# A retention layer and its MLP: every fourth weight block's low parts are made by an accumulating transfer

## The chip, the cores and the metric

The kernel runs on one core of a Trainium2 chip. The metric is device time in microseconds (us) of one launch. The core has five engines that run side by side and wait for one another by semaphores: TensorE (PE in the profile, PEld for its weight loads), VectorE (DVE), ScalarE (ACT), GpSimd (POOL) and SyncE (SP). Sixteen DMA engines move data; a transfer is started by an instruction in the queue of SP, ACT or POOL.

## The reference

With `DEPTH = 1` the program is one retention layer and one squared-ReLU MLP, on 256 tokens of width 2048 in float32:

```python
hn = rmsnorm(x, norm1)
q, k, v, g = split(hn @ w_in)            # 8 heads, 256 wide (q, k), 512 wide (v, g)
q, k = rotary(q), rotary(k) * DK ** -0.5
o = decayed causal attention of q, k, v in chunks of 64 positions
o = head_norm(o, gn_gain, center=True) * silu(g)
x = x + o @ w_out
x = x + square(relu(rmsnorm(x, norm2) @ w_up)) @ w_down    # 8192 wide
out = rmsnorm(x, final_norm)
```

All weights together are 256 blocks of 1 MiB, and each is read once.

## The kernel before, in words

The result has float32 accuracy although TensorE is fed numbers of type float32r. So each weight block is split in a rounded part and a residue: `wh` is the block rounded to float32r by ScalarE (line 59), `wl` is the raw block minus `wh`, by VectorE (line 60). The activations are split likewise, and each product is three matmul passes: `wh` with the activations' high part, `wl` with their high part, `wh` with their low part.

`load_block` does this for one block. SP starts one transfer of 1 MiB into `raw` (128 partitions x 2048 numbers, three buffers in rotation). The block is split in two halves of 128 x 1024; each half has its own `wh` and `wl`, of which there are four buffers each. So the split of half h can begin when TensorE has finished with half h - 4, that is when it starts on half h - 3. Only the first four blocks (head 0's gates) are loaded and split in pieces, with `lead`.

Two loops use the blocks. `proj_cols` (queries and keys, `w_up`) holds the weights stationary: a half is 2 row tiles x 4 column groups, with one matmul of 512 columns on `wh` (line 82) and one of 256 on `wl` (line 83) in each. `proj_rows` (gates, values, `w_o`, `w_down`) holds the activations stationary: a half is 12 matmuls of 512 columns, on `wh` (line 97), on `wl` (line 98), and again on `wh` (line 101). With `late=4`, in the very last projection, the last four row tiles (two blocks, four halves) are kept back and used accumulator by accumulator, so that all four halves are needed within the first twelve matmuls.

The order is: for each of 8 heads four blocks of gates, four of queries and keys, four of values; then two times 16 blocks of `w_o`; then two times 32 blocks of `w_up` and 32 of `w_down`. Between the blocks stand the rest of the layer: `mix` (scores times values), `turn` (transposes, split into `ys` by line 147), the norms. GpSimd does little: the first sums of squares, the reciprocal roots (line 143), and it starts two transfers, the residual `x` (2 MiB, line 325) and `fnorm` (1 MiB, line 392). `x` can start only when the buffers that it takes over are free, at the last head's `turn` after block 4 of `w_o`.

The instructions of each engine run in the order in which the scheduler of the framework has put them, which need not be the order of the code.

Of the kernel before, what the change touches and what calls it, by code (L numbers as in the profile page):

```python
# [9 lines left out]
F32 = mybir.dt.float32  # L10
F32R = mybir.dt.float32r
AF = mybir.ActivationFunctionType
ALU = mybir.AluOpType
PSUM = bass.MemoryType.PSUM

P = 128
T = 256
D = 2048
# [7 lines left out]
EPS = 1e-6  # L26
# [3 lines left out]

@with_exitstack
def trunk_kernel(ctx: ExitStack, tc: tile.TileContext, io, out):
    """One retention layer and its squared-ReLU MLP.

    Every weight product is three float32r passes over exact 12-bit parts (w = wh + wl,
    x = xh + xl): wh*xh + wh*xl + wl*xh, accumulated in float32.
    """
    nc = tc.nc

    cp = ctx.enter_context(tc.tile_pool(name="cp", bufs=1))  # L40
# [3 lines left out]
    def bank(name):  # L44
        return ps.tile([P, 512], F32, tag="bank", name=name)

    # ---- weights: a block of 1 MiB, loaded whole and split in two halves; or, row tile by
    # row tile, with lead(row tile) before each ----
    def load_block(src, rows, cols, lead=None):
        raw = wp.tile([P, 2048], F32, tag="raw", name="raw", bufs=3)  # L50
        if lead is None:
            nc.sync.dma_start(raw, src)
        parts = []
        for s in range(2):
            wh = wp.tile([P, 1024], F32R, tag="wh", name="wh", bufs=4)
            wl = wp.tile([P, 1024], F32R, tag="wl", name="wl", bufs=4)
            r = raw[:, s * 1024 : (s + 1) * 1024]
            if lead is None:
                nc.scalar.copy(wh, r)  # L59
                nc.vector.tensor_sub(wl, r, wh.bitcast(F32))  # L60
            for k in range(rows // 2):
                sl = slice(k * cols, (k + 1) * cols)
                if lead is not None:
                    row = s * rows // 2 + k
                    lead(row)
                    nc.sync.dma_start(r[:, sl], src[:, row * cols : (row + 1) * cols])
                    nc.scalar.copy(wh[:, sl], r[:, sl])  # L67
                    nc.vector.tensor_sub(wl[:, sl], r[:, sl], wh[:, sl].bitcast(F32))  # L68
                parts.append((wh[:, sl], wl[:, sl]))
        return parts  # L70

    # weights stationary: acc[o][n, t] (xh) and acc[o][n, T + t] (xl) over the rows of w,
    # o = 0..3 blocks of 128 columns
    def proj_cols(src, xs, accs, fillers=()):
        for g in range(KT // 4):
            parts = load_block(src[g], 4, 512)
            for j, (wh, wl) in enumerate(parts):
                kt = 4 * g + j
                for o, acc in enumerate(accs):
                    c = slice(o * P, (o + 1) * P)  # L80
                    both = xs[:, kt].rearrange("p a t -> p (a t)")
                    nc.tensor.matmul(acc, wh[:, c], both, start=(kt == 0), stop=False)  # L82
                    nc.tensor.matmul(acc[:, :T], wl[:, c], xs[:, kt, 0, :], start=False, stop=(kt == KT - 1))  # L83
            for f in [f for at, f in fillers if at == g]:
                f()

    # activations stationary: accs[b][c][t, n] over nk row tiles, two token blocks; the last
    # `late` row tiles go to one accumulator after another, with done(b, c) behind each
    def proj_rows(blocks, per, xs, accs, nk, after=(), late=0, done=None, lead=None):
        nch = len(accs[0])  # L90
        kept = []
# [26 lines left out]
                if done:  # L118
                    done(b, c)

# [1 line left out]
    xs = cp.tile([P, KT, 2, T], F32R, tag="xs", name="xs")  # L122
    xr = cp.tile([P, KT, T], F32, tag="ys", name="xr", padded_shape=[P, VT * 2, T])
    norm1 = cp.tile([P, KT], F32, name="norm1")
# [6 lines left out]
    nc.vector.memset(ones, 1.0)  # L131
    nc.vector.memset(mhalf, -0.5)

    # while the first loads are under way: the activation table, and the tensor engine's clock
    warm = cp.tile([P, 1], F32, name="warm")
    nc.scalar.activation(warm, ones[:, 0:1], AF.Silu)
    pw = bank("pw")
# [1 line left out]
        nc.tensor.matmul(pw[:, :P], ones, ones, start=True, stop=True)  # L139

    def rsqrt(r, v):
        """r = v ** -0.5 for [P, 1] tiles."""
        nc.gpsimd.tensor_tensor(r, v, mhalf, op=ALU.pow)

    def split_scaled(dst, src, scale):
        """dst[:, 0] + dst[:, 1] = src * scale, scale [P, 1]."""
        nc.scalar.activation(dst[:, 0, :], src, AF.Copy, scale=scale)
        nc.vector.scalar_tensor_tensor(
            dst[:, 1, :], src, scale, dst[:, 0, :].bitcast(F32), op0=ALU.mult, op1=ALU.subtract
        )  # L150

    with tc.tile_pool(name="ap", bufs=1) as ap:
        # x transposed, times norm1, in two parts; sums of squares by token
        sq = ap.tile([P, 4, T], F32, name="sq")
        sqs = ap.tile([P, T], F32, name="sqs")
        cosr = ap.tile([P, T], F32, name="cosr")
# [3 lines left out]
        def load_x(k0, n):  # L160
            ks = slice(k0, k0 + n)
            nc.sync.dma_start(xr[:, ks], io["xT"][:, ks])
            for k in range(k0, k0 + n):
                split_scaled(xs[:, k], xr[:, k], norm1[:, k : k + 1])

        def lead_x(k):
            """x ahead of the first weights: row tile by row tile, then four at once."""
            if k < 4 or k % 4 == 0:
                load_x(k, 1 if k < 4 else 4)

# [30 lines left out]
            nc.vector.tensor_mul(cosr, cosr, rsrow)  # L201
            nc.vector.tensor_mul(sinr, sinr, rsrow)

# [1 line left out]
        st = {}  # L205

        def gates(h, after, lead=None):
# [38 lines left out]
            st["v"] = v  # L246

        def scores(h):
            """Decayed scores, keys on partitions: columns 0..255 keys 0..127, 256..383 keys 128..255."""
            qk = st["qk"]  # L250
            pst = bank("pst")
            for b in range(NB):
                q = slice(b * P, T)
                to = slice(0, T) if b == 0 else slice(T, T + P)
                for i in range(2):
                    nc.tensor.matmul(
                        pst[:, to], qk[:, 1, i, b * P : (b + 1) * P], qk[:, 0, i, q], start=(i == 0), stop=(i == 1)
                    )
            sd = ap.tile([P, 384], F32, tag="sd", name="sd")
            sh = ap.tile([P, 384], F32R, tag="sh", name="sh")  # L260
            sl = ap.tile([P, 384], F32R, tag="sl", name="sl")
            nc.vector.tensor_mul(sd[:, :T], pst[:, :T], dec[:, h])
            nc.vector.tensor_mul(sd[:, T:384], pst[:, T:384], dec[:, h, :P])
            nc.scalar.copy(sh, sd)
            nc.vector.tensor_sub(sl, sd, sh.bitcast(F32))
            st["s"] = sh, sl
# [49 lines left out]
                nc.sync.dma_start(dec, io["dec"])  # L316
            values(h, [(1, lambda h=h: scores(h))])

# [1 line left out]
        acc0 = [[bank("acc_o") for _ in range(2)] for _ in range(NB)]  # L320
        proj_rows(io["w_o"][0], 2, ys, acc0, VT, [(1, lambda: mix(H - 1)), (4, lambda: turn(H - 1))])

# [1 line left out]
    x = mp.tile([P, NB, D], F32, name="x")  # L324
# [4 lines left out]
    ms2 = mp.tile([P, NB], F32, name="ms2")  # L329
# [10 lines left out]
        )  # L340

    def partial_sum(b):
        """ms2 = the first three sums + D * EPS"""
        m = ms2[:, b : b + 1]
        nc.vector.tensor_scalar(m, ss[:, b, 0:1], ss[:, b, 1:2], D * EPS, op0=ALU.add, op1=ALU.add)
        nc.vector.tensor_add(m, m, ss[:, b, 2:3])
# [40 lines left out]
            nc.tensor.matmul(psr[:, b * P : (b + 1) * P], ones, dg2[:, b], start=True, stop=True)  # L387
        nc.vector.tensor_copy(rsrow2, psr[:, :T])

# [1 line left out]
    fnorm = mp.tile([P, D], F32, name="fnorm")  # L391
    nc.gpsimd.dma_start(fnorm, io["final_norm"])
    rs3 = mp.tile([P, NB], F32, name="rs3")
# [21 lines left out]
    for fh in range(2):  # L415
        hs = cp.tile([P, VT, 2, T], F32R, tag="ys", name="hs")
        for c in range(8):
            acc = [bank("acc_u") for _ in range(4)]
            proj_cols(io["w_up"][8 * fh + c], x1s, acc, [(1, second_norm)] if fh == 0 and c == 0 else ())
            for o in range(4):  # L420
                t = mp.tile([P, T], F32, tag="t", name="t", bufs=3)
                s = mp.tile([P, T], F32, tag="s", name="s", bufs=3)
# [7 lines left out]
        for half in range(2):  # L430
            acc = [[bank("acc_d") for _ in range(2)] for _ in range(NB)]
            last = fh == 1
            proj_rows(
                io["w_down"][fh][half], 2, hs, acc, VT,
                late=4 if last and half == 1 else 0,
                done=(lambda b, c: finish(b, half, c)) if last else (lambda b, c: add_residual(acc, half, b, c)),
# [1 line left out]


def _tables():  # L440
    """Rotary and decay tables: functions of the shapes alone."""
    f = np.float32
    inv = f(10000.0) ** (-np.arange(0, DK, 2, dtype=f) / f(DK))
    ang = np.arange(T, dtype=f)[None, :] * inv.astype(f)[:, None]
    cos, sin = np.cos(ang).astype(f), np.sin(ang).astype(f)
    lg = np.log1p(-np.exp2(-5.0 - np.arange(H, dtype=np.float64)))
    j, i = np.arange(P)[:, None], np.arange(T)[None, :]
    seen = (j // CHUNK) <= (i // CHUNK)
    dist = np.abs(i - j)
    dec = np.exp(lg[None, :, None] * dist[:, None, :]) * seen[:, None, :] * DK**-0.5  # L450
    return cos, sin, np.ascontiguousarray(dec.astype(f))


def _blocks(w, rows, cols):
    """[K, N] -> [N / cols, K / (128 rows), 128, rows, cols], each block contiguous."""
    k, n = w.shape
    w = w.reshape(k // (P * rows), rows, P, n // cols, cols).transpose(3, 0, 2, 1, 4)
    return np.ascontiguousarray(w).reshape(n // cols, k // (P * rows), P, rows * cols)
# [44 lines left out]
```

## Time and profile before

| what | value |
|---|---|
| time, median of 2 runs | 1492.38 us (1492.07 to 1492.69) |
| span of the profiled execution, first to last instruction | 1491.0 us |
| median less span (what lies around the span) | 1.4 us |
| TensorE matmuls, busy | 1471.6 us (99%) |
| VectorE, busy | 852.9 us (57%) |
| ScalarE, busy | 675.8 us (45%) |
| GpSimd, busy | 40.3 us (3%) |
| SP's transfers | 274.05 MB, 52.2% of the 16 DMA engines' time |

No time of the profiled execution other than its span is recorded, so sums are made against the span and 1.4 us are added. "Busy" counts the time in which an instruction of that engine is running; a matmul's end is modelled, and matmuls overlap, so the distance from start to start tells the pace. "idle before <- releaser" names what an engine waited for.

### The profile page before, as it was taken

To read this page: it belongs to the slowest core of one execution; us is meant where nothing else is said; L and a number is where in the kernel's file an instruction comes from. 1 tells how busy PE (TensorE), PEld (TensorE's weight loads), DVE (VectorE), ACT (ScalarE), POOL (GpSimd) and SP (SyncE) were. 2 spreads that over 40 slices of the span, in tenths; PEclk is the share of its full clock that TensorE was granted. 3 is DMA by queue.
4 is the path that set the end of the run, shared out by engine and by line. 5 is a ranking of instruction groups with operands and counts; after the bars stand their busy time and mean duration, and the time that the engine had idled before them with its cause. 6 is when DMAs were issued, how large, how long until landed. Compare 5 with 4: busy or idle time off the path is not lost.

```text
span 1491.0 us, 17881 instructions
## 1 busy us (share of the span) xinstructions
PE 1471.6 (99%) x7172; PEld 1233.2 (83%) x7172; DVE 852.9 (57%) x1099; ACT 675.8 (45%) x870; POOL 40.3 (3%) x48
## 2 busy tenths in 40 slices
PE   7999999999999999999999999999999999999997
PEld 5888888888888888888888888888888888888885
DVE  8656565656565656546466566544446566554645
ACT  5444444444444444434345455533334555443332
POOL 6000000000000000000000000000000000000000
PEclk8999999999999999999999999999999999999999
DMA  6654454454445445655555555555555555555552
GB/s 235 225 187 182 170 198 170 170 188 179 173 174 191 172 174 191 254 198 175 192 175 192 178 189 190 181 194 196 192 185 189 194 176 195 180 189 195 198 185 98
DMA packets 42260, 278.35 MB, mean 187 GB/s; under 512 B 5056, under 2 KB 5952, under 8 KB 9408
## 3 DMA queue, kind: packets, MB, share of 16 engines
q1 hardware_dynamic: 41616, 274.05, 52.2%
q0 software_dynamic: 416, 3.15, 0.5%
q8 instruction: 56, 0.92, 0.2%
q14 instruction: 28, 0.23, 0.0%
q10 hardware_dynamic: 144, 0.01, 0.0%
HBM read 275.09 MB, written 2.10 MB: 186 GB/s over the span
## 4 chain that ended last, share of the span: by engine, by line
PE 96%; DVE 1%; DMA 1%; issue 1%; ACT 0%; POOL 0%; SPq 0%; POOLq 0%; ACTq 0%; DVEq 0%
PE acc_u L82 16%; PE acc_qk L82 8%; PE acc_u L83 8%; PE acc_d L101 8%; PE acc_d L97 8%; PE acc_d L98 8%; PE acc_qk L83 4%; PE acc_v L101 4%; PE acc_v L97 4%; PE acc_v L98 4%; PE acc_o L97 4%; PE acc_o L101 4%; PE acc_g L101 4%; PE acc_o L98 4%; PE acc_g L98 4%; PE acc_g L97 4%
## 5 line engine op out<-in xcount | busy, mean ns | idle before, releaser
L60 DVE TENSOR_TENSOR wl<-raw,wh 128x1024 fp32r<-128x1024 f32 x504 | 615.6, 1224 | 600.9 <-ACT wh L59 600.8
L59 ACT CAST wh<-raw 128x1024 fp32r<-128x1024 f32 x504 | 529.8, 1051 | 703.6 <-PE acc_d L101 204.4
L82 PE MATMUL acc_u<-x1s,wh 128*128 128x512 f32 x1024 | 362.1, 398 | 0.0
L83 PE MATMUL acc_u<-x1s,wl 128*128 128x256 f32 x1024 | 287.8, 281 | 0.0
L82 PEld LDWEIGHTS acc_u<-x1s,wh 128*128 128x128 f32 x1024 | 192.5, 188 | 47.4
L97 PE MATMUL acc_d<-wh,hs 128*128 128x512 f32 x512 | 200.0, 391 | 0.0
L98 PE MATMUL acc_d<-wl,hs 128*128 128x512 f32 x512 | 199.9, 390 | 0.0
L83 PEld LDWEIGHTS acc_u<-x1s,wl 128*128 128x128 f32 x1024 | 192.2, 188 | 0.0
L82 PE MATMUL acc_qk<-xs,wh 128*128 128x512 f32 x512 | 182.1, 398 | 0.0
L101 PE MATMUL acc_d<-wh,hs 128*128 128x512 f32 x512 | 160.8, 393 | 0.0
L83 PE MATMUL acc_qk<-xs,wl 128*128 128x256 f32 x512 | 143.9, 281 | 0.0
L82 PEld LDWEIGHTS acc_qk<-xs,wh 128*128 128x128 f32 x512 | 96.3, 188 | 23.1
L98 PEld LDWEIGHTS acc_d<-wl,hs 128*128 128x128 f32 x512 | 96.1, 188 | 22.2 <-DVE wl L60 0.3
L101 PEld LDWEIGHTS acc_d<-wh,hs 128*128 128x128 f32 x512 | 96.2, 188 | 20.8
L97 PEld LDWEIGHTS acc_d<-wh,hs 128*128 128x128 f32 x512 | 96.2, 188 | 20.4
L98 PE MATMUL acc_g<-wl,xs 128*128 128x512 f32 x256 | 101.9, 398 | 7.5 <-DVE wl L68 7.5
L97 PE MATMUL acc_g<-wh,xs 128*128 128x512 f32 x256 | 101.9, 401 | 0.5 <-ACT wh L67 0.5
L101 PE MATMUL acc_g<-wh,xs 128*128 128x512 f32 x256 | 102.1, 399 | 0.0
L97 PE MATMUL acc_v<-wh,xs 128*128 128x512 f32 x256 | 100.8, 394 | 0.0
L101 PE MATMUL acc_v<-wh,xs 128*128 128x512 f32 x256 | 100.6, 393 | 0.0
L97 PE MATMUL acc_o<-wh,ys 128*128 128x512 f32 x256 | 100.6, 393 | 0.0
L98 PE MATMUL acc_o<-wl,ys 128*128 128x512 f32 x256 | 100.0, 391 | 0.0
(96 smaller groups left out, 1279.5 us busy)
## 6 DMA issues: line engine op xcount, KB each, us to landing
raw<-in_w_up SPq DMA_DIRECT2D x64, 1024.0 KB, 4.9
raw<-in_w_down SPq DMA_DIRECT2D x64, 1024.0 KB, 4.9
raw<-in_w_qk SPq DMA_DIRECT2D x32, 1024.0 KB, 4.9
raw<-in_w_v SPq DMA_DIRECT2D x32, 1024.0 KB, 4.9
raw<-in_w_o SPq DMA_DIRECT2D x32, 1024.0 KB, 4.9
raw<-in_w_g SPq DMA_DIRECT2D x28, 1024.0 KB, 4.9
raw<-in_w_g SPq DMA_DIRECT2D x16, 256.0 KB, 6.3
x<-in_x POOLq DMA_DIRECT2D x1, 2048.0 KB, 10.4
```

Of the source, the lines that this page charges most:

```text
L59: nc.scalar.copy(wh, r)
L60: nc.vector.tensor_sub(wl, r, wh.bitcast(F32))
L82: nc.tensor.matmul(acc, wh[:, c], both, start=(kt == 0), stop=False)
L83: nc.tensor.matmul(acc[:, :T], wl[:, c], xs[:, kt, 0, :], start=False, stop=(kt == KT - 1))
L97: nc.tensor.matmul(accs[b][c], xs[:, kt, 0, t], wh[:, n], start=(kt == 0), stop=False)
L98: nc.tensor.matmul(accs[b][c], xs[:, kt, 0, t], wl[:, n], start=False, stop=False)
L101: nc.tensor.matmul(accs[b][c], xs[:, kt, 1, t], wh[:, n], start=False, stop=(kt == nk - 1))
```

## The change

The fourth, eighth, twelfth block and so on (blocks 8, 12, ..., 256 of the 256, since block 4 is loaded with `lead`) makes `wl` in another way: ScalarE writes the raw half times -1, rounded to float32r, into `wl`, and GpSimd starts a transfer that adds the raw half onto it, tile to tile within the core's own memory. These are 63 blocks, the last of each group of four: 126 halves. The negation reads `raw`, not `wh`. The other 378 halves are split as before. The diff, without the comments that it also drops:

```diff
+    count = [0]
+
     def load_block(src, rows, cols, lead=None):
+        count[0] += 1
+        by_dma = lead is None and count[0] % 4 == 0
         raw = wp.tile([P, 2048], F32, tag="raw", name="raw", bufs=3)
...
             if lead is None:
                 nc.scalar.copy(wh, r)
-                nc.vector.tensor_sub(wl, r, wh.bitcast(F32))
+                if by_dma:
+                    nc.scalar.activation(wl, r, AF.Copy, scale=-1.0)
+                    nc.gpsimd.dma_start(out=wl, in_=r, accum_op=ALU.add)
+                else:
+                    nc.vector.tensor_sub(wl, r, wh.bitcast(F32))
```

In the changed file the cast stands on line 63, the negation on line 65, the transfer on line 66; lines behind are moved by 8. On SP nothing is moved; on PE four rows in `w_down`'s last blocks are.

GpSimd's queue before, from the first norm (line 143, `rs`) over the eight heads (`rv`, two in each) to the end:

```order
L143 TENSOR_TENSOR rs<-ms,mhalf 128x1 x2
L143 TENSOR_TENSOR rv<-ve,mhalf 128x1 x16
L325 DMA x<-in_x 128x2x2048
L392 DMA fnorm<-in_final_norm 128x2048
L143 TENSOR_TENSOR rs_5808<-ms_5171,mhalf 128x1 x2
L143 TENSOR_TENSOR rs_5813<-ms_5171,mhalf 128x1 x2
```

The same queue in the changed kernel, from the seventh head on (line 151 is the old 143, 333 the old 325, 400 the old 392):

```order
L151 TENSOR_TENSOR rv<-ve,mhalf 128x1 x2
L66 DMA wl<-raw 128x1024 x6
L151 TENSOR_TENSOR rv<-ve,mhalf 128x1 x2
L333 DMA x<-in_x 128x2x2048
L66 DMA wl<-raw 128x1024 x2
L400 DMA fnorm<-in_final_norm 128x2048
L66 DMA wl<-raw 128x1024 x12
L151 TENSOR_TENSOR rs_5870<-ms_5225,mhalf 128x1 x2
L66 DMA wl<-raw 128x1024 x64
L151 TENSOR_TENSOR rs_5875<-ms_5225,mhalf 128x1 x2
```

The accumulating transfers stand between GpSimd's roots, and two of them, those of block 8 of `w_o`, stand right behind the 2 MiB of `x`, ahead of `fnorm`.

ScalarE's queue before, in the last head and the first `w_o` blocks (line 291 is in `mix`, line 147 `ys` in `turn`):

```order
L59 CAST wh<-raw 128x1024 x5
L291 ACTIVATE y<-y,rv 128x512
L59 CAST wh<-raw 128x1024
L291 ACTIVATE y<-y,rv 128x512
L59 CAST wh<-raw 128x1024 x5
L147 ACTIVATE ys<-pt,gain 128x256 x4
L59 CAST wh<-raw 128x1024 x28
```

The same place in the changed kernel:

```order
L299 ACTIVATE y<-y,rv 128x512 x2
L63 CAST wh<-raw 128x1024 x6
L155 ACTIVATE ys<-pt,gain 128x256 x4
L65 ACTIVATE wl<-raw 128x1024
L63 CAST wh<-raw 128x1024
L65 ACTIVATE wl<-raw 128x1024
L63 CAST wh<-raw 128x1024 x7
L65 ACTIVATE wl<-raw 128x1024
```

In `proj_rows` the negation of a half stands ahead of its cast (77 of the 126); in `proj_cols` it stands behind it (48, and one in the last `w_down` projection). At `w_o`'s block 8 it stands behind the four `ys`.

ScalarE's queue before, from the last `w_up` group to the end:

```order
L424 COPY s<-acc_u 128x256
L428 CAST hs<-s 128x256
L59 CAST wh<-raw 128x1024
L427 ACTIVATE s<-t 128x256
L428 CAST hs<-s 128x256
L59 CAST wh<-raw 128x1024 x58
L410 ACTIVATE x<-x,rs_5813 128x512 x4
```

The end of that queue in the changed kernel:

```order
L65 ACTIVATE wl<-raw 128x1024
L63 CAST wh<-raw 128x1024
L65 ACTIVATE wl<-raw 128x1024
L63 CAST wh<-raw 128x1024 x7
L65 ACTIVATE wl<-raw 128x1024
L63 CAST wh<-raw 128x1024
L65 ACTIVATE wl<-raw 128x1024
L63 CAST wh<-raw 128x1024
L418 ACTIVATE x<-x,rs_5875 128x512 x4
```

The last two halves of the program, both among the four that are kept back, are made by the accumulating transfer.

## Rows read from the trace of the kernel before

**Rows 1.** The page, part 1: busy time of each engine.

```profile
PE 1471.6 (99%) x7172; PEld 1233.2 (83%) x7172; DVE 852.9 (57%) x1099; ACT 675.8 (45%) x870; POOL 40.3 (3%) x48
```

**Rows 2.** The chain that ended last, share of the span by engine.

```profile
PE 96%; DVE 1%; DMA 1%; issue 1%; ACT 0%; POOL 0%; SPq 0%; POOLq 0%; ACTq 0%; DVEq 0%
```

**Rows 3.** Waits of TensorE's weight loads: us in total, times, longest.

```profile
PEld acc_g L98 <- DVE wl L68: 9.9, 6, 4.4
...
PEld acc_d L98 <- DVE wl L60: 0.3, 1, 0.3
```

**Rows 4.** Groups of instructions: busy us, mean ns of one, idle before.

```profile
L60 DVE TENSOR_TENSOR wl<-raw,wh 128x1024 fp32r<-128x1024 f32 x504 | 615.6, 1224 | 600.9 <-ACT wh L59 600.8
L59 ACT CAST wh<-raw 128x1024 fp32r<-128x1024 f32 x504 | 529.8, 1051 | 703.6 <-PE acc_d L101 204.4
```

**Rows 5.** Timeline in `w_down`: start us, length, engine, line, operation.

```profile
1000.17 0.39 PE L98 MATMUL acc_d<-wl,hs 128*128 128x512 f32 x1
...
1000.65 11.31 SPq L52 DMA_DIRECT2D raw<-in_w_down  x3
1000.86 0.39 PE L97 MATMUL acc_d<-wh,hs 128*128 128x512 f32 x1
...
1001.06 1.05 ACT L59 CAST wh<-raw 128x1024 fp32r<-128x1024 f32 x1 [1.69 <-PE acc_d L101]
...
1009.32 0.39 PE L98 MATMUL acc_d<-wl,hs 128*128 128x512 f32 x1
```

**Rows 6.** Timeline in `w_up`.

```profile
787.55 0.40 PE L82 MATMUL acc_u<-x1s,wh 128*128 128x512 f32 x1
...
787.63 1.05 ACT L59 CAST wh<-raw 128x1024 fp32r<-128x1024 f32 x1 [1.78 <-PE acc_u L82]
...
796.26 0.28 PE L83 MATMUL acc_u<-x1s,wl 128*128 128x256 f32 x1
```

**Rows 7.** DMA, first 700 us: packets, MB, share; issues, KB, us to landing.

```profile
q1 hardware_dynamic: 20880, 129.34, 52.0%
q0 software_dynamic: 416, 3.15, 1.2%
...
raw<-in_w_qk SPq DMA_DIRECT2D x32, 1024.0 KB, 4.9
...
x<-in_x POOLq DMA_DIRECT2D x1, 2048.0 KB, 10.4
xr<-in_xT SPq DMA_DIRECT2D x3, 512.0 KB, 6.6
```

**Rows 8.** One load in `w_down`: last three columns are clock, DMA share, GB/s.

```profile
1001.50:1004.80 3.30, 3.30 (x16) 2.68 (x16) 1.23 (x1) 1.61 (x2) 0.00 (x0) 1.00 0.90 318
```

**Rows 9.** The two us after `x` was issued, same columns.

```profile
615.00:616.00 1.00, 1.00 (x6) 0.80 (x5) 1.00 (x3) 0.05 (x2) 1.00 (x2) 1.00 0.00 0
616.00:617.00 1.00, 1.00 (x6) 0.83 (x5) 0.85 (x3) 0.93 (x3) 0.19 (x1) 1.00 0.85 131
```

**Rows 10.** Timeline in `w_o`, around the issue of `x`.

```profile
614.72 0.90 POOL L325 DMA_DIRECT2D x<-in_x  x1 [15.07 <-ACT ys L147]
...
615.99 0.87 ACT L147 ACTIVATE ys<-pt,gain 128x256 fp32r<-128x256 f32 x2 [0.95 <-DVE ys L148]
...
625.16 0.39 PE L98 MATMUL acc_o<-wl,ys 128*128 128x512 f32 x1
```

**Rows 11.** Timeline at the end: TensorE's matmuls on `wl`.

```profile
1466.73 0.39 PE L98 MATMUL acc_d<-wl,hs 128*128 128x512 f32 x1
...
1469.48 0.39 PE L98 MATMUL acc_d<-wl,hs 128*128 128x512 f32 x1
...
1471.76 0.39 PE L98 MATMUL acc_d<-wl,hs 128*128 128x512 f32 x1
...
1472.73 0.51 PE L98 MATMUL acc_d<-wl,hs 128*128 128x512 f32 x1
```

## The prediction, on record before the changed kernel ran

> **What bounds the kernel now.** I read the busy shares first: TensorE is busy for 1471.6 of 1491.0 us [rows 1], and the chain that ended last is 96% TensorE [rows 2]. So no more than some 19 us could be had from any change of the other engines, and only where TensorE waits for them. Next I asked where it does wait. Its weight loads waited 9.9 us for residues at line 68, which is head 0's gates, the blocks that the change leaves alone; for the residues of line 60, the ones that it takes from VectorE, they waited once, 0.3 us [rows 3]. VectorE's 616 us on them [rows 4] are hidden: **there is nothing to win**, and the question is what the new path costs.
>
> For that the slack has to be read. In `w_down` a half h - 3 starts at 1000.86, and at 1001.06 ScalarE begins the cast of half h, because the buffers of half h - 4 have just come free [rows 5]. The residue of half h is first read at 1009.32 [rows 5]: three halves of 2.75 us and one matmul later. Before, cast and subtraction take 1.05 + 1.22 us [rows 4] of that. In `w_up` the same two points are 787.55 and 796.26 [rows 6].
>
> **The change part by part.**
>
> *Removed:* 126 subtractions of 1.224 us, 154 us of VectorE [rows 4]. They lie beside TensorE's work; the gain on the path is at most the one wait of 0.3 us [rows 3], and that one comes back below.
>
> *Added on ScalarE:* 126 negations. The trace has no such instruction; the nearest is the cast of the same shape, 1.051 us [rows 4], and I take it, in all 132 us. ScalarE goes from 676 to some 810 us; it idles 1.69 us before a cast [rows 5] and runs three halves ahead of TensorE, which covers 1.05 us in two of eight halves. Cost on the path: none. Without that cover it would be up to 132 us.
>
> *Added on GpSimd and the DMA engines:* 126 transfers of 512 KiB. The time from the end of a negation to the landing has three parts.
>
> - Start: GpSimd's issue of `x` took 0.90 us, and its first data moved in the window 616 to 617, not before 616 [rows 9, 10]: 1.3 to 2.3 us after 614.72. I take 1.7.
> - Data, called D: SP's transfers moved 129.34 MB in 52.0% of 700 us [rows 7], 355 GB/s while moving; GpSimd's 3.15 MB in 1.2%, 375 GB/s. 512 KiB are 1.4 to 1.5 us in one pass. An adding transfer reads two tiles and writes one, and none is in the trace. Lower end: one pass, 1.4 us. Middle: two reads in turn, 2.8 us. Upper end: reads and write in turn, 4.2 us; nothing in the rows excludes still more. I take D = 2.8, since a plain transfer, which also reads and writes, gets by with one pass and so seems to do both at once.
> - Landing: a load issued at 1000.65 has done its data by 1004.8 [rows 8] and lands 4.9 us after issue [rows 5, 7]: 0.75 us, taken as 0.8.
>
> As a check on the size I weigh a rule of the Trainium skill. Its page "Collectives: The Full Stack", section "The bandwidth ceiling: the fold count and why AG ≠ RS ≠ AR", says that an add in a transfer halves the rate because it reads two sources on one ring, with some 31 GB/s for one engine's plain copy; 16 engines at half of that would give an estimate of 2.1 us for 512 KiB. No run here shows it; it agrees with two reads being the price, and by it the sum would be about 1498.
>
> Now the path, in `w_down`. The residue buffer is free when the last matmul on `wl` ends, 1000.17 + 0.39 = 1000.56 [rows 5], so half A's negation, ahead of its cast, ends at about 1001.65, and data can move from 1003.3. But the load issued at 1000.65 [rows 5] is moving from 1001.5 on and holds the engines for 0.90 x 3.3 = 3.0 us [rows 8]. Half B's negation ends 2.75 us after A's and its data queue behind A's. The engines then work without a gap from 1001.5: load and A are done by 1001.5 + 3.0 + 2.8 = 1007.3, landed 1008.1, needed 1009.32; B is done at 1010.1, landed 1010.9, needed 1012.07. **Both arrive 1.2 us early.** B arrives late when 1001.5 + 3.0 + 2D + 0.8 > 1012.07, that is **above D = 3.4 us**. In `w_up` the negation stands behind the cast: both end at 787.63 + 2.1 = 789.73, data from 791.4, beyond the load; A lands at 795.0 (needed 796.26), B at 797.9 (needed 799.1). There too D = 3.4 is the edge. So 61 of the 63 blocks cost nothing, and the cover is 1.2 us.
>
> *Freed later:* `raw` is now held until B has landed, 1010.9 in place of about 1006.1 (B's cast begins 2.75 us after the one at 1001.06, and 1.05 + 1.22 us follow [rows 4, 5]), so SP's next load starts 4.8 us later. It lands 4.9 us after, at 1015.8; its cast is due three blocks (16.5 us) after 1000.6, at 1017.1. Cost none; behind it on SP wait only loads that are not due. GpSimd's roots (`rv`, `rs`) stand behind triggers whose negation is ready some 7 us before TensorE needs the half; cost none.
>
> *First exception, `x`:* block 8 of `w_o` has its triggers right behind `x` in GpSimd's queue, and these share one queue of transfers. `x` is issued at 614.72 and lands 10.4 us later, 625.1 [rows 7, 10], its data ending at about 624.3. Half A's negation ends near 618 (behind the four `ys` that end at 616.86 [rows 10]), but its data start only at 624.3 and end at 627.1 alone, 629.1 beside a load; landed 627.9 to 629.9, needed at 625.16 [rows 10]. B follows 2.8 us behind, needed at 627.9. TensorE waits 3 to 5 us; I take **4.0 us**.
>
> *Second exception, the end:* the last block's halves are kept back, and TensorE comes to them within its first twelve matmuls. Third half: buffer free at 1466.73 + 0.39, negated 1468.2, data from 1469.9, landed 1473.5; needed at 1471.76 [rows 11]. Fourth: free at 1469.87, negated 1470.9, data from 1472.6, landed 1476.3; it was read at 1472.73, 0.3 us late already [rows 3, 11]. TensorE, and with it the tail, ends **3.5 us** later.
>
> Sum: 1491.0 + 4.0 + 3.5 = 1498.5 of span, with 1.4 around it **1499.9, say 1500 us** (+0.5%). With D = 1.4 the exceptions shrink to about 2 us each: 1496.5. With D = 3.4 they are 5 each: 1502.5; a little lateness in some blocks gives 1510.
>
> **The rivals.**
>
> *The add is slower than two reads* (ends slower). Point of decision: D above 3.4 us. Each block then loses 2(D - 3.4), as TensorE waits for B, all later halves stand unchanged, and the next adding block comes with the same slack. At D = 4.2: 63 x 1.6 = 101 us and 10 for the exceptions: about 1602. Twice the two reads, D = 5.6: 63 x 4.4 = 277: about 1780. For it: no row shows an add, and the cover is small. Against: the plain transfers run reads and writes at once.
>
> *Late landing with fast data* (ends slower, by little): a fixed delay as in the 6.6 us of a 512 KiB load in the busy start [rows 7]. With 0.9 for the issue that is 7.5 us. From the negation's end to the need there are 1009.32 - 1001.65 = 7.7 us in `proj_rows`, but 796.26 - 789.73 = 6.5 in `proj_cols`; its 24 blocks lose 1.0 us each: 1491.0 + 24 + 10 + 1.4, about 1526.
>
> *Nothing is seen:* `x` is no hindrance, since packets of one queue may overtake, and the end's wait vanishes in the tail's other work: 1492 to 1494.
>
> *Faster:* only if VectorE's 154 us were on the path; rows 3 leave 0.3 us. The gain would end at 1490.
>
> **How the numbers follow.** Forecast 1500: 0.47, own range 1495 to 1510. Nothing seen: 0.07. Slow add: 0.28 at around 1602, 0.09 far above. Late landing 1526: 0.08. Faster: 0.01. The range goes from 1491 to 1640: that leaves out the far slow add and the upper part of the near one, some 0.15 in all. Two per cent of 1492.4 are 30 us, about what a measurement of this kernel can tell from no change; so same is forecast and nothing seen, with the 0.03 of the slow add that lies just above its edge and the lower part of the late landing, 0.04: 0.61; slower 0.38; faster 0.01.
>
> **What would show it.** Right: 126 transfers `wl<-raw` of 512 KB on GpSimd's queue, landing 5 to 6.5 us after issue; waits of TensorE for them at two places only, block 8 of `w_o` and the last block, 3 to 5 us each; VectorE near 700 us, ScalarE near 810; the clock at 1.00 in the middle of the span, as in rows 8 and 9. Wrong: a wait of equal length at each fourth block, on the second half's `wl`. Then D follows from the wait, and if transfers land late though the DMA engines are idle, it is the delay and not the data.

## The result and the profile after

The changed kernel takes **1510.86 us** (median of 2 runs, 1509.03 to 1512.69) against 1492.38: 1.0124 times the time before (95% interval 1.0106 to 1.0143). That is 18.5 us more, inside two per cent, but more than twice the 7.6 us forecast. The profiled run took 1512.69 us, with a span of 1510.9.

The page of the changed kernel, parts 1, 3, 4, 5 and 6 (busy us; chain; groups with busy us, mean ns, idle before; queues with packets, MB, share; issues with KB and median us to landing):

```profile
PE 1480.0 (98%) x7172; PEld 1235.6 (82%) x7172; DVE 701.8 (46%) x973; ACT 794.9 (53%) x996; POOL 147.8 (10%) x174
...
q0 software_dynamic: 18560, 69.21, 23.0%
...
PE 85%; DMA 8%; issue 4%; DVE 1%; ACT 1%; SPq 0%; POOLq 0%; POOL 0%; ACTq 0%; DVEq 0%
...
L66 POOL DMA_DIRECT2D wl<-raw x126 | 108.4, 860 | 1285.5 <-ACT wl L65 1224.9
...
L65 ACT ACTIVATE wl<-raw 128x1024 fp32r<-128x1024 f32 x126 | 133.3, 1058 | 75.6 <-PE acc_d L106 28.5
...
wl<-raw POOLq DMA_DIRECT2D x126, 512.0 KB, 6.0
```

VectorE fell from 852.9 to 701.8 us and ScalarE rose from 675.8 to 794.9, as worked out. But the chain, 96% TensorE before [rows 2], is now 85% TensorE and 8% DMA (the whole time of the transfers that stand on it, not what they cost). The waits of TensorE's weight loads (us in total, times, longest) say where:

```profile
PEld acc_d L106 <- DMA wl<-raw: 8.0, 4, 3.1
PEld acc_o L106 <- DMA wl<-raw: 4.4, 2, 3.9
PEld acc_v L106 <- DMA wl<-raw: 3.9, 7, 0.9
...
PEld acc_u L91 <- DMA wl<-raw: 0.4, 2, 0.3
```

Where there was one wait of 0.3 us [rows 3] there are now 15, on 126 transfers. To see what each costs I set the start of the n-th of the 7172 weight loads in this trace beside the n-th before, from the first instruction of each. TensorE's lateness grows in steps, and between them it stands still:

| place (its time before) | late by, ahead and behind, us |
|---|---|
| start | 0 to 0.5 |
| values, last block of heads 1 to 7 (153 to 578) | 0.5 to 3.4, seven steps of 0.4 to 0.9 |
| `w_o`, block 8 (624.93) | 3.4 to 7.2 |
| the 6 us behind it, at half clock | 7.2 to 10.1 |
| `w_down`, one block (1031.08) | 10.1 to 11.6 |
| `w_down`, one block (1387.77) | 11.5 to 13.3 |
| last `w_down` projection, its first adding block (1409.74) | 13.2 to 16.2, and 17.7 with the clock |
| the last block (1471.54) | 17.7 to 19.0 |

With 0.9 us in the tail this is the 19.9 us between the spans. **Eleven adding blocks of 63 pay besides the last; the other 51 cost next to nothing.** Four of those were late too, by 0.4 us at most (block 12 of `w_o` and three in `w_up`); their waits come to 0.9 us. What sets the eleven apart is seen in the time from issue to landing. The issues of `wl` in the windows 571 to 580 (values, head 7), 620 to 634 (`w_o`, block 8), 1011 to 1020 (a quiet block of `w_down`) and 1416 to 1424 (the last projection), last column:

```profile
wl<-raw POOLq DMA_DIRECT2D x2, 512.0 KB, 8.6
...
wl<-raw POOLq DMA_DIRECT2D x2, 512.0 KB, 10.7
...
wl<-raw POOLq DMA_DIRECT2D x2, 512.0 KB, 6.2
...
wl<-raw POOLq DMA_DIRECT2D x2, 512.0 KB, 9.3
```

The quiet block's 6.2 us are within the forecast's 5 to 6.5; the others are 2.4 to 4.5 us later. The timeline of SP's and GpSimd's issues shows why, at head 7's values and in the last projection (start us, length, engine):

```profile
569.35 0.33 SPq L56 DMA_DIRECT2D raw<-in_w_o  x1
...
571.58 0.33 SPq L56 DMA_DIRECT2D raw<-in_w_o  x1
...
572.71 0.86 POOL L66 DMA_DIRECT2D wl<-raw  x1 [17.76 <-ACT wl L65]
575.46 0.86 POOL L66 DMA_DIRECT2D wl<-raw  x1 [1.89 <-ACT wl L65]
...
1412.87 0.33 SPq L56 DMA_DIRECT2D raw<-in_w_down  x1
...
1416.95 0.33 SPq L56 DMA_DIRECT2D raw<-in_w_down  x1
1417.21 0.87 POOL L66 DMA_DIRECT2D wl<-raw  x1 [21.51 <-DVE ms L353]
```

In the quiet block the last two loads are issued 5.4 us apart (1005.33 and 1010.77), the first is through, and the second has 1.3 us of lead over the first add (1012.07). At the values **two** loads stand ahead of the add, issued 2.2 us apart. In the last projection the first load, issued at 1412.87, landed at 1417.7, before the add could move data; but VectorE's residual and sum-of-squares work had kept the raw tiles, so the second is issued only 0.26 us before the add, and all of its 1 MiB goes ahead. From 1417.6 to 1421.5 no queue but SP's moves data (packets, MB, share of the 16 engines):

```profile
q1 hardware_dynamic: 108, 0.88, 96.0%
```

There the add was also started late: ScalarE's negation stands behind the cast of its own half, and the trigger comes 5.7 us before TensorE begins that half (1417.21 and 1422.95), where the quiet block's comes 7.1 before (1012.07 and 1019.22). At block 8 of `w_o` it is the 2 MiB of `x` that go ahead. The two single blocks of `w_down` are another thing; the row GB/s of the DMA view from 1033 to 1046, in 40 slices:

```profile
GB/s 0 0 277 101 126 328 403 429 429 454 378 265 202 189 214 214 189 214 214 240 214 202 202 239 214 202 164 50 13 13 13 13 13 13 13 13 0 0 0 0
```

For 2.6 us only 13 GB/s move, a sixteenth of the 202 to 240 of the slices before, so that one of the 16 DMA engines is left: it still has its rows of the block's second add to do, and the landing waits for it. It was behind already in the load ahead, which landed 7.4 us after issue instead of some 5. In runs 3, 4 and 6 this block does not pay, and one at 1119 (time before) does.

### The profile page after: what moved, and what is told of

Same layout as the page of the kernel before. It is cut to its first block, busy times and chain, and to the rows that moved or that the text cites. A ratio compares the mean times of both kernels' runs of the same rounds, so it can differ in the third digit from the quotient of the medians.

```text
span 1510.9 us, 18329 instructions
## 1 busy us (share of the span) xinstructions
PE 1480.0 (98%) x7172; PEld 1235.6 (82%) x7172; DVE 701.8 (46%) x973; ACT 794.9 (53%) x996; POOL 147.8 (10%) x174
## 4 chain that ended last, share of the span: by engine, by line
PE 85%; DMA 8%; issue 4%; DVE 1%; ACT 1%; SPq 0%; POOLq 0%; POOL 0%; ACTq 0%; DVEq 0%
PE acc_u L90 16%; PE acc_u L91 8%; PE acc_qk L90 7%; PE acc_d L106 6%; PE acc_d L109 6%; PE acc_d L105 6%; DMA wl<-raw 5%; PE acc_g L106 4%; PE acc_g L109 4%; PE acc_g L105 4%; PE acc_qk L91 4%; PE acc_o L106 3%; PE acc_o L105 3%; PE acc_o L109 3%; PE acc_v L106 3%
## 5 line engine op out<-in xcount | busy, mean ns | idle before, releaser
L68 DVE TENSOR_TENSOR wl<-raw,wh 128x1024 fp32r<-128x1024 f32 x378 | 461.3, 1224 | 669.2 <-ACT wh L63 669.1
L66 POOL DMA_DIRECT2D wl<-raw x126 | 108.4, 860 | 1285.5 <-ACT wl L65 1224.9
L65 ACT ACTIVATE wl<-raw 128x1024 fp32r<-128x1024 f32 x126 | 133.3, 1058 | 75.6 <-PE acc_d L106 28.5
```

Source lines behind the costliest of these rows:

```text
L65: nc.scalar.activation(wl, r, AF.Copy, scale=-1.0)
L66: nc.gpsimd.dma_start(out=wl, in_=r, accum_op=ALU.add)
```

## The experiments

Lines are those of the changed kernel; times are medians, the interval that of the ratio to the kernel before, measured on the same chip. Theory of the places, to begin with: an add costs nothing unless something holds its transfer up. Rival: each adding block costs something, through ScalarE, the traffic or the raw tile that is held longer.

**1. Negation without the transfer.**

```diff
-                    nc.gpsimd.dma_start(out=wl, in_=r, accum_op=ALU.add)
+                    nc.vector.tensor_add(wl, r, wl.bitcast(F32))
```

> The 63 blocks keep ScalarE's negation, but VectorE adds the raw tile onto it (126 additions in place of the 126 transfers); the result is that of the changed kernel. Theory of the places (the loss of 18.5 us arises where the transfer is late: block 8 of w_o 6.7 with the clock behind it, the first adding block of the last w_down 4.4, the values' last blocks 3.0, the end 1.2, two single late transfers 3.3): 1492 to 1494 us, since ScalarE is hidden. Rival, pressure (ScalarE's 133 us more, or the added traffic, cost something in every block): if it is ScalarE, 1500 to 1510.

Measured 1492.14 us, ratio 0.9997 (0.9988 to 1.0007). ScalarE is as busy as in the changed kernel (795.1 us) and costs nothing.

**2. The transfer beside the path.** VectorE makes `wl`; negation and add go to a tile `ng`. To find room the run leaves out six heads' decay tables.

```diff
-                    nc.scalar.activation(wl, r, AF.Copy, scale=-1.0)
-                    nc.gpsimd.dma_start(out=wl, in_=r, accum_op=ALU.add)
+                    nc.vector.tensor_sub(wl, r, wh.bitcast(F32))
...
+                    nc.scalar.activation(ng, r, AF.Copy, scale=-1.0)
+                    nc.gpsimd.dma_start(out=ng, in_=r, accum_op=ALU.add)
```

> VectorE makes all residues as before the change; the negation and the adding transfer of every fourth block are still made, onto a tile that nobody reads. To find room, only two heads' decay tables are loaded and used, so this part of the computation is changed. The raw tile is held until the transfer has read it. Theory of the places: 1492 to 1495 us, since nobody on the path waits for the transfer. Rival, pressure of traffic or of the held raw tile: 1500 to 1511, most of the loss still there.

Measured 1493.99 us, 1.0009 (1.0000 to 1.0019). The traffic and the held tile cost 1.4 us by the ratio (0 to 2.8), though here the transfers take longer (median 8.7 us to landing). What costs is that TensorE waits for `wl`.

**3. Ten blocks back to VectorE.**

```diff
+        by_dma = by_dma and count[0] not in (24, 36, 48, 60, 72, 84, 96, 104, 244, 256)
```

> Ten of the 63 blocks go back to VectorE: the values' last blocks of heads 1 to 7, block 8 of w_o, the first adding block of the last w_down, and the last block. 53 blocks keep the transfer. Theory of the places: what is left is 0.5 of the start and some 3 us of single late transfers, 1493 to 1497 us. Rival, pressure in every block: 53/63 of 18.5 us stay, 1508.

Measured 1496.2 us, 1.0025 (1.0014 to 1.0035): 53 blocks with the transfer lose 4 us, 10 lost the other 14.7. TensorE's matmuls wait for transfers in two blocks of `w_down` only, both single ones as above:

```profile
PE acc_d L107 <- DMA wl<-raw: 2.1, 2, 1.3
```

**4. Block 8 of `w_o` alone back** (`and count[0] != 104`).

> Only block 8 of w_o, whose triggers stand behind x in GpSimd's queue, goes back to VectorE. Theory of the places with the clock behind the wait: 3.9 us of wait and 2.8 us of half clock go, 1504 us (1502.5 to 1506). If the clock's fall has another cause: 1507. Rival, pressure in every block: below 0.5 us gained, 1510.

Measured 1502.28 us, 1.0066 (1.0049 to 1.0083): 8.6 us gained by one block of 63, 0.2 more than the range allowed, where its wait was 3.9. Most of the rest is the clock: 2.9 us behind this wait, and 1.5 behind the last projection's, where the clock stays up in this run. Windows of the changed kernel around that wait (columns as in rows 8):

```profile
624.00:628.00 4.00, 4.00 (x19) 3.30 (x18) 1.14 (x1) 1.57 (x2) 1.29 (x2) 1.00 1.03 348
628.00:632.00 4.00, 0.67 (x3) 0.20 (x2) 1.31 (x2) 1.04 (x1) 0.00 (x0) 0.90 1.01 219
...
634.00:636.00 2.00, 2.00 (x6) 1.58 (x5) 0.00 (x0) 0.00 (x0) 0.00 (x0) 0.50 0.97 410
...
638.00:640.00 2.00, 2.00 (x10) 1.65 (x9) 1.23 (x1) 0.34 (x1) 0.00 (x0) 0.99 0.99 356
```

After the wait the granted clock is 0.50, that is 1.2 of 2.4 GHz, and 6 matmuls start in 2 us where 10 do later. In the changed kernel it falls behind the last projection's wait as well:

```profile
1424.00:1428.00 4.00, 2.01 (x6) 1.60 (x7) 1.22 (x1) 0.19 (x1) 0.00 (x0) 0.82 0.87 172
1428.00:1432.00 4.00, 4.00 (x15) 3.21 (x14) 0.47 (x1) 1.05 (x1) 0.00 (x0) 0.76 0.62 215
```

With block 8 gone that wait is still there, 2.2 us in place of 2.6, and in its windows the clock stays:

```profile
1416.00:1420.00 4.00, 1.84 (x8) 1.54 (x9) 1.23 (x1) 0.84 (x1) 0.00 (x0) 1.00 0.99 198
1420.00:1424.00 4.00, 4.00 (x19) 3.27 (x18) 1.23 (x1) 1.25 (x2) 0.00 (x0) 1.00 0.52 178
```

**5. `x` from ScalarE's queue.** The prediction had put block 8's lateness down to GpSimd's queue.

```diff
-    nc.gpsimd.dma_start(x, io["x"].rearrange("(b p) d -> p b d", p=P))
+    nc.scalar.dma_start(x, io["x"].rearrange("(b p) d -> p b d", p=P))
```

and the same for `fnorm`.

> All 63 blocks keep the transfer; only x and fnorm are issued from ScalarE's queue instead of GpSimd's, so that block 8 of w_o does not stand behind x in its queue, while the bytes are the same. If the order in one queue makes the wait: as with the block taken out, 1502 to 1504 us. Rival (the DMA engines are full there anyway, with x and the loads at once, and divide themselves among the queues): the block is late all the same, 1508 to 1511 us.

Measured 1508.54 us, 1.0108 (1.0093 to 1.0123): the rival's number. TensorE still waits 4.7 us in `w_o`. The DMA view from 618 to 634:

```profile
raw<-in_w_o SPq DMA_DIRECT2D x2, 1024.0 KB, 9.3
wl<-raw POOLq DMA_DIRECT2D x2, 512.0 KB, 9.5
fnorm<-in_final_norm ACTq DMA_DIRECT2D x1, 1024.0 KB, 9.3
```

and the window 622 to 630 with a DMA share of 1.01:

```profile
622.00:630.00 8.00, 6.66 (x30) 5.11 (x28) 2.32 (x2) 4.11 (x4) 1.63 (x2) 1.00 1.01 284
```

The engines are full and everything takes 9 us. What counts is not the order in GpSimd's queue but the bytes that are ahead.

**6. `x` and `fnorm` moved into the gap.** One-element copies make them wait for block 9.

```diff
+            if count[0] == 105 and s == 1:
+                nc.vector.tensor_copy(mark, wl[:, 0:1].bitcast(F32))
...
+    nc.vector.tensor_copy(x[:, 0, 0:1], mark)
     nc.gpsimd.dma_start(x, io["x"].rearrange("(b p) d -> p b d", p=P))
```

> All 63 blocks keep the transfer; x and fnorm are issued only when block 9 of w_o has its low parts (one-element copies hold them back), so that block 8's adds are through before x moves. Theory of the bytes ahead (x's 2 MiB and the loads fill the DMA engines before the adds): block 8's wait and the half clock behind it go, 1502 to 1504 us. Rival (block 8 is late for another reason, its negations standing behind the ys on ScalarE): 1507 to 1511 us.

Measured 1505.0 us (1504.22 to 1507.29), 1.0089 (1.0073 to 1.0104): 1 us above the range. Block 8 no longer waits; its adds, with triggers as late on ScalarE as before, landed 4.8 and 4.9 us after issue. But the 3 MiB took longer than the gap, and the wait moved to the next adding block, 12, where TensorE is 3.2 us later by the table's reckoning:

```profile
PE acc_o L109 <- DMA wl<-raw: 2.8, 1, 2.8
```

The window around it has no fall of the clock:

```profile
650.00:655.00 5.00, 2.86 (x12) 2.36 (x13) 1.23 (x1) 0.15 (x1) 0.00 (x0) 1.00 0.58 116
```

So the bytes decide, and of block 8's 7 us nearly 3 went with the clock alone.

**7. More cover by a fifth `wl` buffer and the negation ahead of the cast.**

```diff
-            wl = wp.tile([P, 1024], F32R, tag="wl", name="wl", bufs=4)
+            wl = wp.tile([P, 1024], F32R, tag="wl", name="wl", bufs=5)
...
-                nc.scalar.copy(wh, r)
                 if by_dma:
...
+                nc.scalar.copy(wh, r)
```

> All 63 blocks keep the transfer; the low parts get a fifth buffer and ScalarE negates a half before it casts it, so that the transfer of a block's first half can start one half (2.75 us) earlier and that of its second some 1.3 us earlier. Theory of the thin cover (the values' blocks, the single late transfers in w_down and the first adding block of the last w_down wait because only 1.2 us of cover were there): those 3.0 + 3.3 us go and most of the 4.4; block 8 of w_o behind x keeps 4 to 6.7: 1497 to 1503 us. Rival (these waits are a matter of traffic that grows with every transfer, wherever it starts): 1508 to 1511.

Measured 1527.08 us, 1.0231 (1.0216 to 1.0247): a miss, and by 16 us slower than the change itself. Landing takes 9.4 us in the median. The timeline in `w_up`:

```profile
855.41 0.33 SPq L56 DMA_DIRECT2D raw<-in_w_up  x1
...
855.69 0.86 POOL L65 DMA_DIRECT2D wl<-raw  x1 [19.80 <-ACT hs L436]
```

The add starts some 2.5 us sooner in TensorE's work and meets the load issued 0.28 us before it; in the changed kernel that load had 2.8 us of lead (853.70 against 856.50). In `w_down` the load is even issued 0.03 us behind the add (994.38 and 994.35) and lands first, after 6.4 us against 9.0. The time won at the start was lost in the queue, with waits of matmuls in 11 blocks of `w_up`, up to 0.8 us each, and in 9 of `w_down`.

**8. Negation first, four buffers** (the second edit of run 7 alone).

> The changed kernel with ScalarE's negation written ahead of the cast, but with four buffers for the low parts as before: one of the two edits of the run that had a fifth buffer as well and took 1527 us. Theory of the queue ahead: without the fifth buffer a negation starts at most one cast (1.05 us) sooner, so most adds meet the same loads: 1509 to 1516 us, and it was the fifth buffer that brought the adds to the moment at which two loads are issued. Rival (ScalarE's order makes the loss, since the casts come later): 1525 us.

Measured 1509.29 us, 1.0117 (1.0102 to 1.0132): no change. Run 7's loss came with the fifth buffer, which was not tried alone.

**9. A fourth `raw` buffer** (`bufs=3` to `bufs=4`; the same six decay tables left out).

> As the changed kernel with a fourth raw buffer. To find room, only two heads' decay tables are loaded and used, so this part of the computation is changed. Theory of the queue ahead: a load starts when a raw tile is released, which with four buffers happens at the same moments as with three, so the adds meet the same loads: 1508 to 1512 us. Rival (the raw tile that the add holds makes the loads late): 1494 to 1500 us.

Measured 1509.91 us, 1.0117 (1.0102 to 1.0132): as expected by the transfers ahead; loads were not late for want of buffers.

**10. Every second block** (`count[0] % 2 == 0`).

> Every second block instead of every fourth gets its low parts by the transfer, 126 blocks without head 0's gates. By the measured data times (3.0 us for a load's 1 MiB, 2.8 for each half's add) two blocks then need 2 x 3.0 + 2 x 2.8 = 11.6 us of the DMA engines in the 11.0 us that TensorE takes for two blocks of w_down and 11.3 of w_up: the engines are the bound, some 0.6 and 0.3 us lost for each pair, about 50 us in all, 1540 to 1600 us, DMA share near 1. Rival, cover alone counts (each place twice): 1525 to 1535 us.

Measured 1807.15 us, 1.2118 (1.2098 to 1.2139): a miss, far above both. The share of the DMA engines is only 0.82 to 0.90 between 110 and 1750 us, so they are not full. Of the 315 us, 219 are waits of TensorE's matmuls for `wl`; another 92 are its own busy time (1563.3 us against 1471.6), at a granted clock of 0.94 to 0.98 in these stretches. The page's chain:

```profile
DMA 61%; issue 26%; PE 10%; DVE 1%; POOL 0%; POOLq 0%; SPq 0%; ACT 0%; ACTq 0%; DVEq 0%
```

and the timeline in `w_down`:

```profile
1218.20 0.33 SPq L56 DMA_DIRECT2D raw<-in_w_down  x1
...
1218.94 0.33 SPq L56 DMA_DIRECT2D raw<-in_w_down  x1
...
1219.38 0.86 POOL L66 DMA_DIRECT2D wl<-raw  x1 [8.52 <-ACT wl L65]
```

Two loads now come together, in the 4 us before the adds, in some 110 of the 126 blocks, and landing takes 9.3 us in the median, more than the cover. A raw tile that the adds release late and one that VectorE releases on time come free at once: the delay feeds itself. That last step is read from the timeline; no run tested it.

**11. The second of every four blocks** (`count[0] % 4 == 2`).

> Again 63 or 64 blocks, but the second of every four (2, 6, 10, ...; within w_g, w_qk and w_v always the second block) instead of the fourth. Theory of the places: these blocks don't fall on a values' block behind two loads, nor behind x in GpSimd's queue, nor on the last block; what is left is the start, single late transfers and whatever the last projection's second block meets: 1494 to 1500 us. Rival, the loss goes with the number of transfers: 1510 us.

Measured 1510.35 us, 1.0121 (1.0106 to 1.0136): a miss. The values' waits are gone, but others are there:

```profile
PE acc_u L91 <- DMA wl<-raw: 4.0, 14, 0.7
PE acc_qk L91 <- DMA wl<-raw: 3.8, 1, 3.8
```

One is behind the loads of the constants at the start. The 14 in `w_up` are new, and explained by the next run.

**12. Only the second half, of every second block.**

```diff
+        by_dma = lead is None and count[0] % 2 == 0
...
-                if by_dma:
+                if by_dma and s == 1:
```

> Of every second block only the second half gets its low parts by the transfer, VectorE makes the first half's: again 126 transfers of 512 KiB and as many negations, the same bytes, but one at a time every 11 us in place of two together every 22. Theory of the queue ahead (an add is served only behind the loads that were issued before it, and the second add behind the first; late come those with two loads or x ahead): a lone add ends 2.8 us sooner against its need, so only block 8 of w_o beside x may wait, 2 to 4 us: 1493 to 1499 us. Rival (it is the number of transfers or their bytes that costs): 1508 to 1512 us, and if all three raw tiles being held longer decides, more.

Measured 1512.52 us, 1.0131 (1.0114 to 1.0148): a miss. The values no longer wait, but `w_up` does, 14 times:

```profile
PE acc_u L91 <- DMA wl<-raw: 3.9, 14, 0.5
```

No load stands ahead there. ScalarE's timeline, with TensorE's matmul that waits:

```profile
794.71 1.08 ACT L432 COPY s<-acc_u 128x256 f32<-128x256 f32 x3 [0.83 <-PE acc_u L91]
...
798.80 1.07 ACT L65 ACTIVATE wl<-raw 128x1024 fp32r<-128x1024 f32 x1
...
804.73 0.39 PE L91 MATMUL acc_u<-x1s,wl 128*128 128x256 f32 x1 [0.28 <-DMA wl<-raw]
```

In a projection's second block the negation stands behind the evictions of the projection before (794.71 to 798.90) and ends at 799.87; with 0.3 to the trigger and the shortest landing, 4.5, the half is there at 804.7. It is a **second cause: a trigger that is late on ScalarE**. Most of the change's own blocks, the fourth of each projection, don't meet it; the first adding block of the last projection does, beside its load (above), and so does block 8 of `w_o`, behind the four `ys`.

The same trace holds an add that runs alone, issued at 823.33 and landed 4.5 us later (windows as in rows 8):

```profile
823.30:824.70 1.40, 1.40 (x10) 1.22 (x9) 0.38 (x1) 1.40 (x4) 0.86 (x1) 1.00 0.00 0
824.70:827.60 2.90, 2.90 (x17) 2.26 (x15) 2.32 (x3) 1.15 (x2) 0.00 (x0) 1.00 0.96 181
827.60:828.40 0.80, 0.55 (x4) 0.50 (x4) 0.02 (x1) 0.74 (x1) 0.00 (x0) 1.00 0.00 0
```

Nothing moves for 1.4 us, then the engines are busy for 0.96 x 2.90 = 2.8 us, then nothing.

Runs 11 and 12 left open whether each transfer has a price after all. Three more runs kept many transfers and took away only the places named.

**13. Run 12 without the second blocks of `w_up` and block 8 of `w_o`** (109 transfers left).

> As the run with the second half of every second block, which took 1512.5 where 1493 to 1499 was expected; 17 more blocks go back to VectorE: the second block of each w_up projection (its trace shows TensorE late by some 0.65 us there, 14 times, the negation standing behind the evictions of the projection before on ScalarE) and block 8 of w_o (2.6 of wait and 2.7 of clock). Theory of the late trigger: 1512.5 - 9.1 - 5.3 = 1498 us (1496 to 1500). Rival (the number of transfers or bytes costs in every block): 109 of 126 are left, 1509 us.

Measured 1498.05 us, 1.0039 (1.0024 to 1.0053).

**14. The second half of every fourth block, without block 8 of `w_o`** (62 transfers).

> Of every fourth block the second half alone gets its low parts by the transfer, and block 8 of w_o none: 62 transfers. By the queue ahead, a lone add ends 2.8 us sooner against its need than the second of a pair, so the values' blocks and the single late engines are covered, and the last of four stands behind no evictions; left are the start, the first adding block of the last w_down and the end, a part of 2.6 and 1.2 us: 1493 to 1496 us. Rival (cost per transfer): half of 18.5 less 4, 1499 us or more.

Measured 1494.21 us, 1.0016 (1.0006 to 1.0025). One wait of TensorE for a transfer is left:

```profile
PE acc_d L106 <- DMA wl<-raw: 1.1, 1, 1.1
```

**15. Run 11 without `w_up` and without the early block of queries and keys** (46 blocks left; the expectation counts one too many).

> As the run with the second of every four blocks, which took 1510.35, but the blocks of w_up (14 waits of some 0.63 us there, late triggers) and the first of w_qk (one wait of 3.8 us behind the constants' loads) go back to VectorE: 47 blocks keep both adds. Theory: 1510.35 - 8.9 - 3.9 = 1497.5 us (1496 to 1500). Rival (cost per block): 47 of 64 blocks' share of 18 us, 1505 us.

Measured 1497.33 us, 1.0034 (1.0022 to 1.0046). All three agree with the places and not with a price for each transfer. No version in which TensorE reads what a transfer made beats the kernel before; the nearest, run 14, is 2 us slower and takes 72 us off VectorE, which nobody needs.

## Why the prediction was wrong, point by point

- **Nothing to win, and ScalarE hidden: right.** Run 1 is at 1492.14, and the negation took 1.058 us where 1.051 was taken.
- **The add's three parts: start and data right, landing too long.** In run 12's lone add the first data move 1.7 us after the negation's end (821.97 + 1.06, then 824.7; taken 1.7), the data take 2.8 (taken 2.8), and it lands 4.8 us after the negation's end, where the terms give 5.3: the last term is some 0.3 in place of 0.8. The Trainium skill's "Collectives: The Full Stack", section "The bandwidth ceiling: the fold count and why AG ≠ RS ≠ AR", gave an estimate of 2.1 us from an add's two reads; in direction the trace agrees (one pass would be 1.4), the measured 2.8 decides on the size. The slow add and the late landing are excluded as causes by these figures and by the quiet blocks.
- **"So 61 of the 63 blocks cost nothing, and the cover is 1.2 us": the step that failed.** It was worked out from one place in `w_down` and one in `w_up`, each with a single load ahead of the add, issued 1.3 us or more before it. That is near enough for 51, with less cover: 0.8 us in the quiet `w_down` block (landed 1018.4, TensorE at 1019.2), and in `w_up` the first halves landed between 0.8 us early and 0.2 late. Seven values' blocks have two loads ahead, 2.9 us; the last projection's first adding block has a load issued 0.26 us ahead and a late trigger, 3.0 us (with 1.5 more by the clock); in two blocks of `w_down` one DMA engine was late, 1.5 and 1.8 us. Together some 11 us that the sum did not have. Runs 3 and 4 differ by seven values' blocks, the last projection's and the last block, and by 6.1 us.
- **Block 8 of `w_o`, 4.0 us: right in size, partly by luck, and one term short.** The wait was 3.9, and `x` does go ahead; but the reason given, one shared queue, is not what counts (run 5): it is the bytes of `x` and the loads (runs 5, 6). And the sum had nothing for what a wait leaves behind: 2.9 us at half clock.
- **The end, 3.5 us: mis-sized.** TensorE lost 1.3 there and the tail behind it 0.9. Both halves landed 4.5 us after issue (at 1490.8 and 1493.5), and only the third was late, by 1.2 us. The fourth cost nothing, since the need was read in the order of the kernel before, where TensorE takes it right behind the third [rows 11]. In the changed kernel that matmul stands further back:

```profile
1490.81 0.50 PE L106 MATMUL acc_d<-wl,hs 128*128 128x512 f32 x1 [1.16 <-DMA wl<-raw]
...
1491.85 0.39 PE L106 MATMUL acc_d<-wl,hs 128*128 128x512 f32 x1
...
1493.68 0.39 PE L106 MATMUL acc_d<-wl,hs 128*128 128x512 f32 x1
```

The one at 1491.85 starts without a wait before the fourth half has landed, so it reads another half, of the next accumulator; the fourth's first use is the one at 1493.68.
- **The rival of capacity** (a slower add, counted through cover): its edge at 3.4 us was not tried directly. Run 10 shows that adds can be late in most blocks at D = 2.8 already, once two loads stand ahead of them.

## What to carry to other kernels

A transfer that takes the place of an instruction has no fixed price: count what has been issued in the few us ahead of it on every queue, and how late its trigger is, at each place of its own kind, not at one quiet place. Starting it sooner helps only if it does not meet a load there. And put small shares of work on such a path where the trace shows one load ahead and an unhindered trigger: by run 14 most of the loss goes with half of the transfers.

## What the runs showed of the hardware that was not expected

- A load issued 0.26 us before an add, on another queue, moves its data first (the last projection above), and in run 7 even one issued 0.03 us behind it. That fits the starts: a load's data move some 0.85 us after issue [rows 5, 8], an add's after 1.4 (run 12). The add's landing rises from 4.5 us alone and 6.2 behind a load with 1.3 us of lead to 8.6 behind two loads and 9.3 behind one issued 0.26 us ahead.
- TensorE's clock fell to 0.50 after the wait of 3.5 us in `w_o`, and to 0.82 and 0.76 in the two windows of 4 us behind one of 2.6 us in the last projection; it stayed at 1.00 after waits of 2.8 (run 6) and 2.2 us (run 4). What decides between them is open.
- One DMA engine's worth of data ended 2.6 us behind the rest in the changed kernel's block at 1034. An instruction transfer of 16 KB stands in the trace shortly before; such transfers stand before other adds too, without harm, so the cause is open.
